# Adding every expert block's rows to X on the tensor engine in the second mixture-of-experts layer

## The chip, the cores and the metric

The kernel runs on one core of one Trainium2 chip as one launch. The core has a tensor engine (PE, with its weight loads shown apart as PEld), a vector engine (DVE), a scalar engine (ACT), GpSimd (POOL) and a sync engine (SP) that here only issues DMAs; POOL issues the indirect DMAs. The metric is device time in microseconds (us), the median of three timed runs; lower is better. Besides those runs there is one profiled execution, and all durations below come from its trace.

## The reference, cut to what matters

Two transformer blocks run one after the other on 512 tokens of width 1024. The first block has two layers, and each ends in a mixture of experts with 32 experts, of which every token uses two. In the first layer 768 rows (512 tokens and 256 context rows) go through the experts, in the second layer 512.

```python
def expert_block(args):
    xblk, e = args
    return (jax.nn.silu(xblk @ w_gate[e]) * (xblk @ w_up[e])) @ w_down[e]
...
return jnp.zeros((n_tok + 1, d), h.dtype).at[row_tok].add(yb * row_w[:, None])[:n_tok]
...
x = x + g2 * hier_moe(h2.reshape(b * s, d), *moe).reshape(x.shape)
```

So each expert multiplies its tokens' rows by three float32 matrices (1024x512, 1024x512, 512x1024, 6.3 MB together), the result is scaled by the routing weight, and the two results of each token are added to the residual stream X after a multiplication by the column g2.

## The kernel before, in words

`moe(l, n_tok, fg, side_work)` is called once per layer. The experts are ranked by load. A block holds 128 rows: either one expert with up to 128 rows (a single), or two experts with 64 rows each (a pair), which run as two column halves of PE at `tile_position` (0, 0) and (0, 64). In the second layer there are 18 blocks: block 0 is a pair, 1 to 4 are singles (`MANY = 4`), 5 to 17 are pairs. The list `turn` sets the order in which they run; the loop over `e` goes through it.

For each block, `expert` gathers the rows with an indirect DMA (`xg`), transposes them on PE (`xt`), and then runs three stages: gate, up and down. Each has four chunks. A chunk loads one 512 KB `raw` tile per expert (issued by SP, in a ring of reused buffers) and multiplies it in float32, which the trace shows as two instructions for one product: 8 instructions in a chunk of a pair and 4 in a chunk of a single, so 96 or 48 in a block. `h` of the gate and up stages (`eh`) is transposed on PE into `ht` for the down stage. In the loop, iteration e issues gate of e, gather and transposes of e+1, down of e-1, and up of e.

After the down stage of a block, `rows_of` scales the two result banks into `ey` (ACT) and `put` scatters the rows to a DRAM tensor `yd` by indirect DMA (line 985). Near the end `add_rows` reads `yd` back in four 1 MB pieces `yr` (line 1031), adds the two rows of each token (DVE, line 1034), transposes them on PE and adds them to X (DVE, line 1042). The last two blocks (`own`) are not sent through DRAM: `own_parts` makes `ysh` and `ysl` (a value and its rest, both in the rounded float32 form `fp32r`) and a one-hot matrix `own` of slot by token; `add_own` multiplies 128 columns of `ysh` and of `ysl` by the one-hot matrix, two PE products of 128x512 into a `tp` bank, and DVE adds the bank to X (line 1022). It does so for 8 column groups k, so 16 products per block.

Side work is woven in by `hooked`, called after each chunk: `self.hook = (n, generator)` runs n steps of the generator there. `self.pe` records an order for PE when `pe_turn` is set: each PE instruction then stands behind the one written before it; otherwise a scheduler may place it elsewhere. In iteration 12 (`pause`) stands `overflow`, a loop behind a branch that runs only for experts that hold more rows than their slots.

The FFN that follows takes over the products of the last block.

Of the kernel before, what the change touches and what calls it, by code (L numbers as in the profile page):

```python
# [59 lines left out]
class Kernel:  # L60
# [212 lines left out]
    def setup(self, ctx):  # L273
# [5 lines left out]
        self.wrings = [(pool("wsp", 3), 3, [0])]  # L279
        self.more_raw = (13, 13)  # L280
        self.open_x(ctx, 2)
# [502 lines left out]

    def overflow(self, l, n_tok, h2d, Yd, p2, x):

# [6 lines left out]
        with tc.If(nb > 0):  # L793
            with tc.For_i(0, nb, 1) as i:
                with ExitStack() as st:
# [30 lines left out]
                    *_, pss = self.expert(p2, l, [bass.ds(e, 1)], x, queue=nc.gpsimd)  # L826
                    y = self.rows_of(p2, pss, wt[:, 0:1])
                    nc.gpsimd.indirect_dma_start(
                        out=Yd, out_offset=bass.IndirectOffsetOnAxis(ap=row[:, 0:1], axis=0),
                        in_=y, in_offset=None, bounds_check=2 * n_tok - 1, oob_is_err=False)  # L830

# [6 lines left out]
    def moe(self, l, n_tok, fg, side_work):  # L838
# [7 lines left out]
        h2d = self.dram.tile([n_tok, D], F32, name=f"h2d{l}")  # L846
        Yd = self.dram.tile([2 * n_tok, D], F32, name=f"yd{l}")
        with ExitStack() as st:
# [4 lines left out]
            with ExitStack() as st1:  # L853
# [108 lines left out]

                turn = [0]
                for i in range(nb - 1 - MANY[l]):
                    turn += [1 + i] * (i < MANY[l]) + [1 + MANY[l] + i]
                pair = n1 - 2 * (1 + MANY[l])
                ranks = lambda b: [0, 1] if b == 0 else [b + 1] if b <= MANY[l] else [2 * b + pair, 2 * b + pair + 1]
                ysc = []
                with ExitStack() as st2:
# [23 lines left out]

                    def own_parts(e, pss, hot):

                        w = swt(turn[e])
                        if e == own[0]:
                            YS = self.split_tile(p2, [128, CH], "ys", 1)
                        elif len(segs) == 1:
                            YS = self.split_tile(self.turn_of(self.wrings)[0], [128, CH], "w")  # L1000
                        else:
                            YS = Split(*[p2.tile([128, CH], F32R, name=self.uid("ys"), tag="xt", bufs=2) for _ in (1, 2)])
                        for b in range(2):
                            o = slice(512 * b, 512 * b + 512)
                            nc.scalar.activation(YS.hi[:, o], pss[b], AF.Copy, scale=w)
                            V.scalar_tensor_tensor(YS.lo[:, o], pss[b], w, YS.hi[:, o].bitcast(F32), op0=ALU.mult, op1=ALU.subtract)
                        tokf = p2.tile([128, 1], F32, name=self.uid("tokf"), tag="tokf", bufs=2)
                        V.tensor_copy(tokf, stok(turn[e]))
                        V.tensor_scalar(hot, toks, tokf, None, op0=ALU.is_equal)
                        return YS, hot  # L1010

# [34 lines left out]
                    own = range(nb - 2, nb)  # L1046
                    rows = add_rows()
                    start(0)
                    last = V.memset(xg[1], 0.0)
                    nc.gpsimd.memset(xg[2], 0.0)  # L1050
                    for e in range(nb):
                        if e == 0:
                            with tc.issue_after(last.ins), tc.issue_after(after_q):
                                next(ex[e])
                        else:
                            if e == own[1]:
                                self.hook, self.pe_turn = (1, rows), True
                            next(ex[e])
                        if e + 1 < nb:
                            start(e + 1)  # L1060
                        if e:
                            pss = next(ex[e - 1])
                            if e == own[1]:
                                mine = own_parts(e - 1, pss, self.own or p2.tile([128, n_tok], F32R, name="own", tag="ey", bufs=self.eys))
                                self.hook = (2 if tt > 4 else 1, rows)
                            else:
# [4 lines left out]
                        if e == 2:  # L1071
                            with tc.issue_after(self.split_last):
                                self.extra(pool)

                            z = p2.tile([128, 2, D], F32, name="zero", tag="yr", bufs=2)[:, 0]
                            nc.gpsimd.memset(z, 0.0)
                            for i in own:
                                put(i, z)
                        if e == self.pause:
                            self.overflow(l, n_tok, h2d, Yd, p2, xg[(e + 2) % 3])  # L1080
                            self.pe_last = None
# [3 lines left out]
                    for _ in chain(rows, side_work):  # L1085
                        pass
                    later_adds = len(segs) == 1
                    adds = add_own(mine) if later_adds else iter(())
                    self.hook = (2, adds)
                    pss = next(ex[nb - 1])  # L1090
                    for _ in adds:
                        pass
                    self.hook = None
                    last = own_parts(nb - 1, pss, self.own or p2.tile([128, n_tok], F32R, name="own2", tag="ey", bufs=self.eys))
                    adds = add_own(last) if later_adds else add_own(mine, last)
                    self.in_turn = False
                    del self.rings[1:]
                    if later_adds:
                        self.pe_turn = False
# [1278 lines left out]
```

## Time and profile before

| what | value |
|---|---|
| median of 3 timed runs | 2939.95 us (2939.86 to 2944.88) |
| profiled execution | 2945.97 us |
| span of its trace | 2944.3 us |
| PE busy over the span | 2739.8 us (93%) |
| DMA mean over the span | 218 GB/s |
| mean granted PE clock | 0.970 |

A shown PE duration overlaps the next one, since products are pipelined; where a pace is wanted it is the distance between the starts of two rows. All times in the rows count from the start of the span.

### The profile page before, as it was taken

The page shows a single profiled execution, that of the slowest core. Times are in us where ns is not written, and L with a number is a line of the kernel's source. Part 1 is how long each engine was busy: PE and PEld are TensorE (multiplying, and loading weights), DVE is VectorE, ACT ScalarE, POOL GpSimd, SP SyncE. Part 2 cuts the span into 40 slices and gives each one's busy share as a digit, 9 for nine tenths or more (in the row PEclk, how much of TensorE's full clock was granted, in tenths as well). Part 3 has the DMA queues.
Part 4 walks back from the last instruction along what each step waited for, and adds up shares of the span by engine and source line. Part 5 has one row for each costly group of instructions (what it writes and reads, how often), then busy time and mean ns, then how long its engine had stood idle before and what let it go on. Part 6 is the DMA issues. An engine that isn't in the chain of part 4 may idle for free. (4 is left out here: it accounts for less than half of the span.)

```text
span 2944.3 us, 35083 instructions
## 1 busy us (share of the span) xinstructions
PE 2739.8 (93%) x12714; PEld 1796.7 (61%) x12714; DVE 1242.4 (42%) x2267; ACT 886.6 (30%) x1421; POOL 430.6 (15%) x431
## 2 busy tenths in 40 slices
PE   7989889999988999989999887999999889999998
PEld 3756644333325889754433323778888777888886
DVE  4884530000025566842100114654337767444335
ACT  3464211110103477310000002333226665333223
POOL 1663110000001100111000001550002230000000
PEclk9999989999999999989999998999999999999999
DMA  7656699999995201289999995333233422232231
GB/s 251 209 191 230 222 352 408 398 398 403 398 409 218 72 31 37 93 318 397 405 412 412 410 414 199 104 123 102 93 103 115 130 58 83 93 97 97 94 96 62
DMA packets 210850, 642.98 MB, mean 218 GB/s; under 512 B 31440, under 2 KB 40752, under 8 KB 209392
## 3 DMA queue, kind: packets, MB, share of 16 engines
q1 hardware_dynamic: 194208, 598.89, 55.1%
q0 software_dynamic: 16464, 41.80, 3.8%
q8 instruction: 101, 1.65, 0.2%
q14 instruction: 77, 0.63, 0.1%
HBM read 623.32 MB, written 36.14 MB: 224 GB/s over the span
## 5 line engine op out<-in xcount | busy, mean ns | idle before, releaser
L1129 PE MATMUL ps<-raw,xt 128*64 128x512 f32 (+1 forms) x2048 | 614.8, 608 | 18.5 <-DMA raw<-exp_w_up 13.1
L171 PE MATMUL ps<-Hh,wl 128*128 128x512 f32 (+1 forms) x1320 | 495.6, 377 | 3.2 <-DVE wl L91 3.1
L170 PE MATMUL ps<-Hl,wh 128*128 128x512 f32 (+1 forms) x1320 | 498.0, 378 | 0.1
L169 PE MATMUL ps<-Hh,wh 128*128 128x512 f32 (+1 forms) x1320 | 495.0, 381 | 2.9 <-ACT Hh L262 2.1
L1129 PEld LDWEIGHTS ps<-raw,xt 128*64 128x64 f32 (+1 forms) x2048 | 201.3, 148 | 373.8 <-issue 264.6
L89 ACT ACTIVATE wh<-raw 128x1024 fp32r<-128x1024 f32 (+1 forms) x224 | 231.6, 1040 | 583.8 <-PE ps L170 477.3
L91 DVE TENSOR_TENSOR wl<-raw,wh 128x1024 fp32r<-128x1024 f32 (+1 forms) x224 | 276.2, 1236 | 206.8 <-ACT wh L89 206.4
L1195 DVE TENSOR_TENSOR eh<-ps,eh 128x512 f32<-128x512 f32 x38 | 26.3, 692 | 758.2 <-PE ps L1129 706.8
L1129 PE MATMUL ps<-raw,ht 128*64 128x512 f32 (+1 forms) x1024 | 307.2, 599 | 5.4 <-issue 2.8
L169 PEld LDWEIGHTS ps<-Hh,wh 128*128 128x128 f32 x1320 | 248.2, 189 | 67.4 <-issue 5.0
L170 PEld LDWEIGHTS ps<-Hl,wh 128*128 128x128 f32 x1320 | 249.2, 189 | 56.1 <-issue 4.2
L171 PEld LDWEIGHTS ps<-Hh,wl 128*128 128x128 f32 x1320 | 248.5, 189 | 51.1 <-DVE wl L91 4.1
L1129 PEld LDWEIGHTS ps<-raw,ht 128*64 128x64 f32 (+1 forms) x1024 | 112.5, 146 | 182.6 <-issue 156.9
L1193 ACT ACTIVATE eh<-ps 128x512 f32<-128x512 f32 x38 | 22.7, 597 | 473.4 <-PE ps L1129 473.4
L413 POOL TENSOR_TENSOR cg<-cg,cp 128x798 f32<-128x798 f32 x60 | 120.9, 2015 | 102.1 <-ACT cp L412 94.3
L1217 ACT ACTIVATE ey<-ps,swt 128x512 f32<-128x512 f32 x64 | 42.9, 686 | 233.1 <-PE ps L1129 230.7
L985 POOL DMA_INDIRECT yd<-ey,srow x32 | 31.9, 995 | 548.1 <-ACT ey L1217 496.0
L169 PE MATMUL ps<-Gh,wh 128*128 128x512 f32 x256 | 101.1, 395 | 0.0
L171 PE MATMUL ps<-Gh,wl 128*128 128x512 f32 x256 | 101.1, 395 | 0.0
L170 PE MATMUL ps<-Gl,wh 128*128 128x512 f32 x256 | 101.1, 395 | 0.0
L1548 DVE TENSOR_TENSOR fs<-ps,fs 128x512 f32<-128x512 f32 x44 | 30.4, 691 | 143.1 <-PE ps L171 142.4
L362 PE MATMUL ps<-raw,sc 128*32 128x512 f32 x384 | 72.9, 643 | 5.2 <-DMA raw<-mod_w 5.2
(738 smaller groups left out, 3950.8 us busy)
## 6 DMA issues: line engine op xcount, KB each, us to landing
raw<-exp_w_gate SPq DMA_DIRECT2D x256, 512.0 KB, 11.0
raw<-exp_w_up SPq DMA_DIRECT2D x256, 512.0 KB, 10.6
raw<-exp_w_down SPq DMA_DIRECT2D x256, 512.0 KB, 10.9
raw<-ffn_w SPq DMA_DIRECT2D x132, 512.0 KB, 3.4
raw<-mod_w SPq DMA_DIRECT2D x96, 512.0 KB, 5.1
yr<-yd POOLq DMA_DIRECT2D x10, 1024.0 KB, 8.4
X<-xT SPq DMA_DIRECT2D x16, 384.0 KB, 7.5
raw<-w_in_ab SPq DMA_DIRECT2D x12, 512.0 KB, 6.8
```

Source lines behind the costliest of these rows:

```text
L89: self.nc.scalar.activation(dst.hi, src, AF.Copy)
L91: self.split_last = eng.tensor_tensor(dst.lo, src, dst.hi.bitcast(F32), ALU.subtract).ins
L169: mm(ps, a.hi, b.hi, start=start, stop=False)
L170: mm(ps, a.hi, b.lo, start=False, stop=False)
L171: mm(ps, a.lo, b.hi, start=False, stop=stop)
L362: nc.tensor.matmul(ps[32 * g:32 * g + 32], self.sc[:, 4 * h + g, 30 - 2 * i:62 - 2 * i], ws[g // 2][:, (g % 2) * 512:(g % 2 + 1) * 512], s ...
L413: nc.gpsimd.tensor_tensor(a, a, t, ALU.add)
L985: ysc.append(nc.gpsimd.indirect_dma_start(out=Yd, out_offset=bass.IndirectOffsetOnAxis(ap=srow(turn[e]), axis=0), in_=y, in_offset=None, b ...
L1129: i = f(*a, **kw).ins
L1195: nc.vector.tensor_tensor(h, ps, h, ALU.mult)
L1217: self.nc.scalar.activation(y[:, 512 * b:512 * b + 512], pss[b], AF.Copy, scale=wt)
L1548: V.tensor_tensor(s, ps, s, ALU.mult)
```

## The change

Only the second layer's experts change. The flag `direct` is set there (one token segment). Then `yd` and `add_rows` don't exist; after the down stage of every block `own_parts` makes `ysh`, `ysl` and the one-hot matrix (one buffer each, `self.own` for the one-hot), and `add_own` is hung on the hook with one step per chunk: 4 steps in the up stage of the next block and 4 in the gate stage after it. The last block's products go to the FFN as before. `pe_turn` is set in the whole loop except around the branch. The ring of `raw` tiles gets 17 instead of 13 buffers in this layer. The four singles stand at places 1, 5, 9 and 13 of the sequence instead of 1, 3, 5 and 7.

```diff
-        self.more_raw = (13, 13)
+        self.more_raw = (13, 17)
...
-        Yd = self.dram.tile([2 * n_tok, D], F32, name=f"yd{l}")
+
+        direct = len(segs) == 1
+        Yd = None if direct else self.dram.tile([2 * n_tok, D], F32, name=f"yd{l}")
...
                 turn = [0]
+                apart = (nb - 1 - MANY[l]) // MANY[l]
                 for i in range(nb - 1 - MANY[l]):
-                    turn += [1 + i] * (i < MANY[l]) + [1 + MANY[l] + i]
+                    single = [1 + i // apart] * (i % apart == 0 and i // apart < MANY[l])
+                    turn += single + [1 + MANY[l] + i]
...
-                    def own_parts(e, pss, hot):
-
-                        w = swt(turn[e])
-                        if e == own[0]:
+                    def own_parts(w, tok, pss, hot, at=None):
+
+                        if at is None:
                             YS = self.split_tile(p2, [128, CH], "ys", 1)
...
                         tokf = p2.tile([128, 1], F32, name=self.uid("tokf"), tag="tokf", bufs=2)
-                        V.tensor_copy(tokf, stok(turn[e]))
+                        V.tensor_copy(tokf, tok)
                         V.tensor_scalar(hot, toks, tokf, None, op0=ALU.is_equal)
                         return YS, hot
...
-                    rows = add_rows()
+                    rows = iter(()) if direct else add_rows()
+                    adds = iter(())
+                    parts_of = lambda e, *a: own_parts(swt(turn[e]), stok(turn[e]), *a)
...
-                            if e == own[1]:
-                                self.hook, self.pe_turn = (1, rows), True
+                            if e == own[1] and not direct:
+                                self.hook = (1, rows)
+                            self.pe_turn = direct or e >= own[1]
                             next(ex[e])
...
                             pss = next(ex[e - 1])
-                            if e == own[1]:
-                                mine = own_parts(e - 1, pss, self.own or p2.tile([128, n_tok], F32R, name="own", tag="ey", bufs=self.eys))
-                                self.hook = (2 if tt > 4 else 1, rows)
+                            if direct:
+                                for _ in adds:
+                                    pass
+                                adds = add_own(parts_of(e - 1, pss, self.own))
+                                self.hook = (1, adds)
...
                         if e == self.pause:
-                            self.overflow(l, n_tok, h2d, Yd, p2, xg[(e + 2) % 3])
+                            for _ in adds:
+                                pass
+                            self.hook, self.pe_turn = None, False
+                            self.overflow(l, n_tok, h2d, Yd, p2, xg[(e + 2) % 3], add if direct else None)
                             self.pe_last = None
...
-                    later_adds = len(segs) == 1
-                    adds = add_own(mine) if later_adds else iter(())
-                    self.hook = (2, adds)
                     pss = next(ex[nb - 1])
                     for _ in adds:
                         pass
                     self.hook = None
-                    last = own_parts(nb - 1, pss, self.own or p2.tile([128, n_tok], F32R, name="own2", tag="ey", bufs=self.eys))
-                    adds = add_own(last) if later_adds else add_own(mine, last)
+                    if direct:
+                        adds = add_own(parts_of(nb - 1, pss, self.own, self.turn_of(self.wrings)[0]))
```

What this does to the order of the engines' instructions, at two places. First PE, where one pair of the second layer ends its up stage and the next begins its gate stage. Before, the transposes of the `h` that has just been finished (`eh`) and of the next rows (`xg`) stand between the first products of the gate stage:

```order
L1129 MATMUL ps_10844<-raw_10871,xt_10646 64x512
L1129 MATMUL ps_10879<-raw_10880,xt_10784 64x512
L1129 MATMUL ps_10936<-ident,eh_10740 128x128 x4
L1129 MATMUL ps_11061<-ident,xg_9343 128x128 x4
L1129 MATMUL ps_10879<-raw_10882,xt_10784 64x512
L1129 MATMUL ps_10879<-raw_10880,xt_10784 64x512
L1129 MATMUL ps_10879<-raw_10882,xt_10784 64x512
L1129 MATMUL ps_11067<-ident,xg_9343 128x128 x4
```

In the change two one-hot products follow every chunk of four rows (8 instructions in the trace), and all transposes stand together at the end of the gate stage, right ahead of the down stage that needs the last of them:

```order
L1152 MATMUL ps_9942<-raw_9979,xt_9828 64x512
L1152 MATMUL ps_9942<-raw_9981,xt_9828 64x512
L1152 MATMUL ps_9942<-raw_9979,xt_9828 64x512
L1152 MATMUL ps_9942<-raw_9981,xt_9828 64x512
L1152 MATMUL ps_9987<-own,ysh_9882 128x512
L1152 MATMUL ps_9987<-own,ysl_9883 128x512
L1152 MATMUL ps_9999<-ident,xg_9343 128x128 x4
L1152 MATMUL ps_10005<-ident,xg_9343 128x128 x4
L1152 MATMUL ps_10012<-ident,eh_9768 128x128 x4
L1152 MATMUL ps_10018<-raw_10020,ht_10011 64x512
```

So 16 products per block have moved into 17 of the 18 blocks, and the down stage now stands directly behind the transposes of its own `h`.

Second DVE, around the same place (`xt` and `ht` are the copies of the transposed rows and of the transposed `h`). Before, the copy `ht` stands behind the two copies `xt`, and nothing is between them:

```order
L1195 TENSOR_TENSOR eh_11348<-ps_11452,eh_11348 128x512
L1173 TENSOR_TENSOR xt_11530<-ps_11531,xshift 128x512
L1173 TENSOR_TENSOR xt_11530<-ps_11537,xshift 128x512
L1202 COPY ht_11543<-ps_11544 128x512
L1195 TENSOR_TENSOR eh_11486<-ps_11590,eh_11486 128x512
```

In the change the addition to X for the last column group and the next block's one-hot matrix stand ahead of them:

```order
L1029 SCALAR_TENSOR_TENSOR X<-ps_10436,mod,X 128x512
L1016 TENSOR_SCALAR own<-acc,tokf_10494 128x512
L1196 TENSOR_TENSOR xt_10450<-ps_10451,xshift 128x512
L1196 TENSOR_TENSOR xt_10450<-ps_10457,xshift 128x512
L1015 CAST tokf_10885<-stok 128x1
L1225 COPY ht_10463<-ps_10464 128x512
L1013 SCALAR_TENSOR_TENSOR ysl_10489<-ps_10470,swt,ysh_10488 128x512
```

So `ht`, for which the down stage waits, has three more instructions ahead of it on DVE.

## Rows read from the trace of the kernel before

**Rows 1.** The page: the span in 40 slices, tenths busy, GB/s.

```profile
PE   7989889999988999989999887999999889999998
PEclk9999989999999999989999998999999999999999
GB/s 251 209 191 230 222 352 408 398 398 403 398 409 218 72 31 37 93 318 397 405 412 412 410 414 199 104 123 102 93 103 115 130 58 83 93 97 97 94 96 62
```

**Rows 2.** Windows of 50 us in the second layer's experts.

```profile
core 0: us, PE busy (x) PEld busy (x) DVE busy (x) ACT busy (x) POOL busy (x), PEclk, DMA share, GB/s
...
1350.00:1400.00 50.00, 49.11 (x185) 20.76 (x182) 7.64 (x12) 3.84 (x6) 4.06 (x4) 1.00 1.02 399
...
1700.00:1750.00 50.00, 43.91 (x147) 13.40 (x145) 3.18 (x5) 3.35 (x5) 3.11 (x4) 1.00 1.02 411
```

**Rows 3.** PE's timeline in the early blocks (start, us, instruction, count, idle before).

```profile
1287.52 15.79 PE L1129 MATMUL ps<-raw,xt 128*64 128x512 f32 x64 [1.95 <-issue]
...
1308.28 0.60 PE L1129 MATMUL ps<-ident,xg 128*128 128x128 f32 x4
1308.72 3.60 PE L1129 MATMUL ps<-raw,xt 128*128 128x512 f32 x8
...
1337.35 0.71 PE L1129 MATMUL ps<-ident,xg 128*128 128x128 f32 x4
1337.99 1.07 PE L1129 MATMUL ps<-raw,xt 128*64 128x512 f32 x2
...
1382.65 7.13 PE L1129 MATMUL ps<-raw,ht 128*128 128x512 f32 x16
1389.72 7.09 PE L1129 MATMUL ps<-raw,xt 128*64 128x512 f32 x32
1397.70 0.75 PE L1129 MATMUL ps<-ident,eh 128*128 128x128 f32 x4 [0.89 <-DVE eh L1195]
...
1445.43 0.75 PE L1129 MATMUL ps<-ident,eh 128*128 128x128 f32 x4 [0.89 <-DVE eh L1195]
```

**Rows 4.** DMA of the window 1300 to 1800 us: queue totals, issues.

```profile
q0 software_dynamic: 4962, 11.41, 5.8%
...
yr<-yd POOLq DMA_DIRECT2D x4, 1024.0 KB, 8.4
```

**Rows 5.** PE's timeline around the end of the last block.

```profile
1753.22 1.11 PE L1129 MATMUL ps<-ident,yr 128*128 128x128 f32 x4 [6.61 <-DVE yr L1034]
...
1787.22 1.94 PE L1129 MATMUL ps<-raw,ht 128*64 128x512 f32 x8 [0.78 <-DVE ht L1202]
1789.09 0.50 PE L1129 MATMUL ps<-own,ysh 128*128 128x512 f32 x1
1789.43 0.40 PE L1129 MATMUL ps<-own,ysl 128*128 128x512 f32 x1
1789.66 0.40 PE L1129 MATMUL ps<-own,ysh 128*128 128x512 f32 x1
1789.90 0.40 PE L1129 MATMUL ps<-own,ysl 128*128 128x512 f32 x1
1790.22 1.94 PE L1129 MATMUL ps<-raw,ht 128*64 128x512 f32 x8
...
1798.90 0.40 PE L1129 MATMUL ps<-own,ysl 128*128 128x512 f32 x1
1801.95 0.47 PE L1129 MATMUL ps<-own,wh 128*128 128x512 f32 x1 [2.65 <-DVE own L1009]
```

**Rows 6.** DVE by line and form, 1280 to 1800 us (busy, mean ns).

```profile
L1173 DVE TENSOR_TENSOR xt<-ps,xshift 128x512 f32<-128x512 f32 x36 | 23.2, 682 | 24.7 <-PE ps L1129 24.7
...
L1202 DVE COPY ht<-ps 128x512 f32<-128x512 f32 x18 | 12.3, 683 | 8.3 <-PE ps L1129 8.3
...
L1022 DVE SCALAR_TENSOR_TENSOR X<-ps,mod,X 128x512 f32<-128x512 f32 x7 | 5.0, 748 | 5.9 <-PE ps L1129 5.9
...
L1009 DVE TENSOR_SCALAR own<-acc,tokf 128x512 fp32r<-128x512 f32 x1 | 0.5, 498 | 0.0
```

**Rows 7.** The timeline at the branch of the overflow loop.

```profile
1619.53 2.06 PE L1129 MATMUL ps<-raw,xt 128*64 128x512 f32 x8 [0.51 <-PEq L793]
...
1626.90 1.94 PE L1129 MATMUL ps<-ident,xg 128*128 128x128 f32 x8 [5.31 <-DMA xg<-h2d,stok]
```

More of the change, by code (lines that the diff above doesn't have):

```diff
@@ L783, in extra, with overflow @@
         self.more = (lst, xl, at)
-    def overflow(self, l, n_tok, h2d, Yd, p2, x):
+    def overflow(self, l, n_tok, h2d, Yd, p2, x, add=None):
         tc, nc = self.tc, self.nc
@@ L826, in overflow @@
                     *_, pss = self.expert(p2, l, [bass.ds(e, 1)], x, queue=nc.gpsimd)
[L827 to L830, printed above, removed]
+                    if add:
+                        add(wt[:, 0:1], tok[:, 0:1], pss)
+                    else:
+                        y = self.rows_of(p2, pss, wt[:, 0:1])
+                        nc.gpsimd.indirect_dma_start(
+                            out=Yd, out_offset=bass.IndirectOffsetOnAxis(ap=row[:, 0:1], axis=0),
+                            in_=y, in_offset=None, bounds_check=2 * n_tok - 1, oob_is_err=False)
     pause = 12
@@ L992, in moe @@
                     nc.gpsimd.iota(toks, pattern=[[1, n_tok]], base=0, channel_multiplier=0, allow_small_or_imprecise_dtypes=True)
-                    def own_parts(e, pss, hot):
-                        w = swt(turn[e])
-                        if e == own[0]:
+                    def own_parts(w, tok, pss, hot, at=None):
+                        if at is None:
                             YS = self.split_tile(p2, [128, CH], "ys", 1)
-                        elif len(segs) == 1:
-                            YS = self.split_tile(self.turn_of(self.wrings)[0], [128, CH], "w")
+                        elif direct:
+                            YS = self.split_tile(at, [128, CH], "w")
                         else:
-                            YS = Split(*[p2.tile([128, CH], F32R, name=self.uid("ys"), tag="xt", bufs=2) for _ in (1, 2)])
+                            YS = Split(*[at.tile([128, CH], F32R, name=self.uid("ys"), tag="xt", bufs=2) for _ in (1, 2)])
                         for b in range(2):
@@ L1046, in moe, with add @@
                     own = range(nb - 2, nb)
-                    rows = add_rows()
+                    rows = iter(()) if direct else add_rows()
+                    adds = iter(())
+                    parts_of = lambda e, *a: own_parts(swt(turn[e]), stok(turn[e]), *a)
+                    def add(*a):
+                        for _ in add_own(own_parts(*a, self.own)):
+                            pass
                     start(0)
@@ L1062, in moe @@
                             pss = next(ex[e - 1])
-                            if e == own[1]:
-                                mine = own_parts(e - 1, pss, self.own or p2.tile([128, n_tok], F32R, name="own", tag="ey", bufs=self.eys))
-                                self.hook = (2 if tt > 4 else 1, rows)
+                            if direct:
[3 more added lines that the diff above has]
+                                self.hook = (1, adds)
+                            elif e == own[1]:
+                                mine = parts_of(e - 1, pss, p2.tile([128, n_tok], F32R, name="own", tag="ey", bufs=self.eys))
+                                self.hook = (2, rows)
                             else:
@@ L1073, in moe @@
                                 self.extra(pool)
[L1075 to L1078, printed above, removed]
+                            if not direct:
+                                z = p2.tile([128, 2, D], F32, name="zero", tag="yr", bufs=2)[:, 0]
+                                nc.gpsimd.memset(z, 0.0)
+                                for i in own:
+                                    put(i, z)
                         if e == self.pause:
-                            self.overflow(l, n_tok, h2d, Yd, p2, xg[(e + 2) % 3])
+                            for _ in adds:
+                                pass
+                            self.hook, self.pe_turn = None, False
+                            self.overflow(l, n_tok, h2d, Yd, p2, xg[(e + 2) % 3], add if direct else None)
                             self.pe_last = None
@@ L1093, in moe @@
                     self.hook = None
-                    last = own_parts(nb - 1, pss, self.own or p2.tile([128, n_tok], F32R, name="own2", tag="ey", bufs=self.eys))
-                    adds = add_own(last) if later_adds else add_own(mine, last)
+                    if direct:
+                        adds = add_own(parts_of(nb - 1, pss, self.own, self.turn_of(self.wrings)[0]))
+                    else:
+                        adds = add_own(mine, parts_of(nb - 1, pss, p2.tile([128, n_tok], F32R, name="own2", tag="ey", bufs=self.eys), p2))
                     self.in_turn = False
                     del self.rings[1:]
-                    if later_adds:
+                    if direct:
                         self.pe_turn = False
```

## The prediction

> **What bounds the kernel now.** I read the slices of the page first [rows 1]: two stretches run at some 400 GB/s, the experts of the two layers. Only the second, from about 1287 to 1799 us, is touched. There both PE and the DMA engines look full, and the question is which of them ends last. The windows [rows 2] answer it: in the late window the DMA engines move 411 GB/s and PE is busy 43.9 of 50 us, in the early window it is 399 GB/s with PE busy 49.1. The granted clock is 1.00 in both (the 2.4 GHz level), so no term below has a clock in it. PE's busy time hides overlap, so I take its pace from starts. In the early blocks, where singles and pairs alternate, the same transposes come back after 1445.43 - 1397.70 = 47.73 us [rows 3]; that is one single and one pair, and within it PE waits only 0.89 us. A pair's 32 instructions of one stage start at 1389.72 and end before 1396.8, the 16 of a single's stage take 1389.72 - 1382.65 = 7.07: both kinds cost PE the same, three stages of some 7.07 plus some 2 us of transposes, **23.87 us a block** (47.73 / 2) [rows 3].
>
> For the DMA engines they are not the same. A pair needs 24 tiles of 524 KB, 12.6 MB, 30.6 us at 411 GB/s; a single half of it, 15.3 us [rows 2]. So pairs are bound by the weights (PE has about 7 us to spare in each), singles by PE. Over the stage PE's own work is 18 x 23.87 = 429.7 us, and the stage lasts from 1287.5 to the last product of block 16's sums at 1799.2, 511.7 us [rows 3, 5]. Some 5 us of that are 16 one-hot products and some 5 the transposes of `yr`, so PE stands still for about 72 us. The stage is bound by the DMA stream, and the change takes bytes from the stream and gives work to PE.
>
> **What it removes.** The four reads of `yd` are 4.2 MB, and all indirect and POOL traffic of the window is 11.41 MB [rows 4]. Of the other 7.2 MB I count half as scatters (one per gather). So 7.8 MB go, 7.8 / 411 GB/s = 19 us of stream. The 6.61 us for which PE waits for the first `yr` [rows 5] go too; in a stage bound by the stream they are no further gain, since the stream runs on meanwhile.
>
> **What it adds to PE.** 17 blocks get 16 products inside the stage; block 17's stay with the FFN, as before. The trace has this very pattern once, in the last down stage [rows 5]: 8 instructions, 4 one-hot products, 8 instructions, from 1787.22 to 1790.22, 3.00 us. The products follow each other at 0.23 to 0.24 us (1789.43, 1789.66, 1789.90). 8 instructions at the pace of the stage (7.07 / 4) are 1.77, so four products cost 1.23 us, of which 4 x 0.235 = 0.94 are streaming and 0.29 the change-over from half-array float32 products to full-array ones and back. In the change a chunk gets two products, so the change-over is paid twice as often: 0.47 + 0.29 = 0.76 us per hook. In the chunks of a single the change-over is shorter: four transposes between its products take 1308.72 - 1308.28 = 0.44 us against 1337.99 - 1337.35 = 0.64 in a pair [rows 3]; I take 0.57 per hook there. Of the 136 hooks (17 x 8), 32 lie in the up and gate stages of the four singles, 5 run in a burst ahead of the branch at DVE's 0.75 us for one addition to X [rows 6], and 99 lie in pairs: 99 x 0.76 + 32 x 0.57 + 5 x 0.75 = 75.2 + 18.2 + 3.8 = **97 us**. Bounds: 17 x 4 x 1.23 = 84 (the price with four products to a hook), and 136 x 0.76 = 103.
>
> At the streaming price the Trainium skill is more generous: "TensorE: Matmul & The Clock Gate", section "Back-to-back issue gap", gives a sustained 131 ns for a product of 512 columns with its weight load, which would make 17 x 16 x 0.131 = 36 us of these products (an estimate from that page). The trace disagrees with it here, at 0.23 to 0.24 us from start to start [rows 5].
>
> **What it moves.** `pe_turn` fixes PE's order, and the transposes for the down stage now stand right ahead of it. After the last one-hot product of a gate stage DVE has to do the addition to X (0.75), the next one-hot matrix (0.50), two `xt` copies (0.68 each) and then `ht` (0.68) [rows 6], with a small cast some 3.35 us, while PE has three groups of transposes (some 0.65 each [rows 3], 1.95). PE waits some 1.6 us for `ht`, with the two signals between the engines. In the pace of 23.87 there is a wait of 0.89 in every second block [rows 3], 0.45 a block, and it goes, because `eh` is then long done. Net 1.15 us in 17 blocks, **20 us**. Bounds: 0.35 a block (the 0.78 that the last block waits for `ht` with DVE free [rows 5]), 6 us, and 2.1 a block if the signals and `xt` wait on each other, 36 us. At the last block the order stays as it is (its transposes already wait twice), some 1.5 us over the pace.
>
> For the first sum in an up stage `ysh` and `ysl` have to be made in the 1.8 us of its first chunk. ACT takes the first result bank before the down stage ends, and the two DVE operations of 0.75 end some 1.7 us after it. I cost this at nothing, and at 0.75 us x 17 = 13 if the cover is short.
>
> At the branch PE waits 0.51 us and then 5.31 for a gather that POOL issues after it [rows 7]. In the change the gate stage of a single (7.07 us) stands ahead of those transposes and covers most of the landing; I take 2.5 us in all, at most the present 8.
>
> Placing the singles apart costs PE nothing, since both kinds take the same PE time; it decides only how long the stream can run ahead. Four more buffers let it run 2.1 MB further ahead. Both cost nothing and, where PE ends last, gain nothing. DVE gets 136 additions (102 us in a stage of 550), ACT works on two banks per block as before; neither is near its limit. POOL loses its scatters, so gathers can only be earlier.
>
> **The sum.** PE's work from 1287.5 on: 429.7 + 97 + 20 + 1.5 + 2.5 = 550.7, which ends at 1838.2 against 1799.2: 39 us later. The stream would need 511.7 - 19 = 493, so PE ends last and the 19 us are lost in its shadow. Behind the stage the FFN's first weights can land and be split while PE still works, where now PE waits 2.65 us at its door [rows 5] with those splits on DVE; I count 2 us of gain. Net +37: 2945.97 + 37 = 2983 us in the profiled execution. Its time is 6.0 us over the median of the runs shown (2939.95), so the forecast for the median is **2977 us**.
>
> **The rivals.**
> 1. *The stream stays the bound.* The products fit into PE's 72 us of standing still, and the 7.8 MB come off the end: 2940 - 19 = 2921 us. For it: 411 GB/s in the late windows [rows 2] and 7 us to spare in each pair. It decides below (493 - 429.7) / 17 = 3.7 us per block for products and waits together. Against it: the products alone cost 4 x 1.23 = 4.9 in the trace [rows 5], and a single has no spare time at all (23.87 of PE against 15.3 of stream). Chance 8%. The page's 131 ns would give this outcome (2.1 us per block); by the measured spacing that page's rule has little weight.
> 2. *Only the cheap part of the costs.* Products at 84 us, the wait for `ht` at 6, no wait at the branch, 4 us gained at the FFN's door: 429.7 + 84 + 6 + 1.5 = 521.2, 9.5 - 4 = 5.5 us later, 2945 us. For it: the scheduler's order today hides most such waits. Against it: the change-over comes with each hook, and the hooks hold one step each. Chance for a result below 2957: 14%, a third of it within 0.2%.
> 3. *More waits.* The fixed order also stalls every up stage on `ysl` (13 us), `ht` costs the upper bound (16 more), the branch stays as it is (5 more): +71, 3011 us. For it: `ysh`, `ysl` and `own` have one buffer each, so nothing can be prepared far ahead. Chance of more than 3000: 11%.
>
> That the products might run elsewhere than planned is excluded by the order shown above.
>
> **Chances and range.** The forecast (2957 to 3000) has 67%, rival 1 8%, rival 2 14%, rival 3 11%. A difference of 0.2%, some 6 us, is about what a measurement of this kernel can tell from none. Faster: rival 1, 8%. Same: the third of rival 2, 5%. Slower: 87%. The range that leaves out rival 1, the low part of rival 2 and the far part of rival 3 is 2948 to 3000.
>
> **What would show it.** In the second layer's experts PE should have no wait for `raw` tiles between the second block and the last, and the stream should fall from 411 to some 201 MB of weights and 4 MB of gathers in 550 us, 370 to 375 GB/s. The distance from one block's down stage to the next should be some 31 us for pairs and 30 for singles, instead of 30.6 and less. Each pair of one-hot products should take 0.7 to 0.8 us out of the flow, and PE should stand 1.2 to 2 us before each down stage on `ht`. If instead the transfers run at 410 GB/s to the end and PE waits for them, rival 1 holds. The prediction fails on the low side if two products cost less than 0.5 us or if the wait for `ht` is hidden by the queue of products, on the high side if a wait ahead of the first sum shows in every up stage.

## The result and the profile after

The changed kernel takes 2965.54 us (median of 4 runs, 2962.17 to 2968.88), the kernel before 2941.89 us beside it (4 runs, 2939.86 to 2944.88): ratio 1.0079, 95% interval 1.0064 to 1.0094. It is slower by 23.6 us; 37 had been forecast, with the right direction and cause but too large a size.

The profiled execution took 2964.15 us, 18.2 more than that of before. In this execution untouched code before 300 us already ran 5.3 us earlier than in that of before, and the same 5.3 us are still there at the routing's last product ahead of the second layer's experts. So 18.2 + 5.3 = 23.5 us is what the changed stretch costs in these two executions; that it comes so close to the 23.6 of the medians is in part luck, since single executions of one kernel differ by more.

The page's slices of the changed kernel (as [rows 1]; tenths busy, GB/s):

```profile
PE   7989799999988999979999998999999889999998
GB/s 258 210 204 211 219 389 406 399 398 404 398 411 170 63 26 60 115 351 403 372 394 362 335 417 145 104 119 103 97 93 126 135 51 82 97 96 100 93 94 63
```

Where the stream ran at 397 to 414 GB/s through the second layer's experts, it now falls to 335 (369 GB/s as the mean from 1284 to 1820 us, where 370 to 375 had been forecast), and most of PE's digits are at 9. A window of 50 us in which the stream is held back, while PE is busy for 48.5 us (the rest is the wait described below):

```profile
core 0: us, PE busy (x) PEld busy (x) DVE busy (x) ACT busy (x) POOL busy (x), PEclk, DMA share, GB/s
1550.00:1600.00 50.00, 48.50 (x180) 18.57 (x180) 16.25 (x24) 3.35 (x5) 0.00 (x0) 1.00 0.92 336
```

PE's waits from 1284 to 1800 us (what it waited for, us in total, times, longest):

```profile
PE ps L1152 <- DVE ht L1225: 24.7, 17, 1.9
PE ps L1152 <- DVE xt L1196: 1.9, 2, 1.5
PE ps L1152 <- DMA xg<-h2d,stok: 0.7, 1, 0.7
PE ps L1152 <- PEq L794: 0.5, 1, 0.5
```

No wait for a `raw` tile is among them. The weight loads (PEld), which overlap PE's work, say the same: from 1290 to 1775 us they wait 9.6 us for `raw` tiles, in the kernel before 68.6 us. So PE ends last. PE's timeline: the first gate product, two chunks of a single, a pair, and the end of the last block:

```profile
1283.59 10.80 PE L1152 MATMUL ps<-raw,xt 128*64 128x512 f32 x36 [1.51 <-DVE xt L1196]
...
1440.22 1.88 PE L1152 MATMUL ps<-raw,xt 128*128 128x512 f32 x4
...
1442.40 1.88 PE L1152 MATMUL ps<-raw,xt 128*128 128x512 f32 x4
...
1487.38 1.05 PE L1152 MATMUL ps<-ident,xg 128*128 128x128 f32 x8
1488.39 0.75 PE L1152 MATMUL ps<-ident,eh 128*128 128x128 f32 x4
1490.64 7.09 PE L1152 MATMUL ps<-raw,ht 128*64 128x512 f32 x32 [1.50 <-DVE ht L1225]
...
1500.04 1.94 PE L1152 MATMUL ps<-raw,xt 128*64 128x512 f32 x8
...
1502.57 1.94 PE L1152 MATMUL ps<-raw,xt 128*64 128x512 f32 x8
...
1520.93 4.51 PE L1152 MATMUL ps<-raw,ht 128*64 128x512 f32 x20 [1.50 <-DVE ht L1225]
...
1817.58 0.40 PE L1152 MATMUL ps<-own,ysl 128*128 128x512 f32 x1
1819.41 0.47 PE L1152 MATMUL ps<-own,wh 128*128 128x512 f32 x1 [1.43 <-DVE own L1016]
...
1822.91 0.79 PE L1152 MATMUL ps<-own,wh 128*128 128x512 f32 x1 [2.33 <-DVE X L1029]
```

The new wait stands ahead of each down stage (`ht`). One pair takes 1520.93 - 1490.64 = 30.29 us. In it a chunk with its two products takes 1502.57 - 1500.04 = 2.53; less 1.77 for the chunk, a hook costs 0.76. Without its 8 hooks and its wait the block would take 30.29 - 8 x 0.76 - 1.50 = 22.7 us. DVE's timeline at the same place shows why `ht` is late:

```profile
1487.58 0.75 DVE L1029 SCALAR_TENSOR_TENSOR X<-ps,mod,X 128x512 f32<-128x512 f32 x1 [1.79 <-PE ps L1152]
1488.25 0.48 DVE L1016 TENSOR_SCALAR own<-acc,tokf 128x512 fp32r<-128x512 f32 x1
1488.64 1.28 DVE L1196 TENSOR_TENSOR xt<-ps,xshift 128x512 f32<-128x512 f32 x2
1489.84 0.15 DVE L1015 CAST tokf<-stok 128x1 f32<-128x1 int32 x1
1489.90 0.68 DVE L1225 COPY ht<-ps 128x512 f32<-128x512 f32 x1
```

PE's last transpose ends at 1489.14, but DVE is on the addition, the one-hot matrix and the two `xt` until 1489.9.

For comparing versions I use one length: from the first gate product to the first product of the last block's sum, the first row of the timeline above and its row with the wait of 1.43. In the changed kernel that is 1819.41 - 1283.59 = 535.8 us; before, from [rows 3] and [rows 5], 1801.95 - 1287.52 = 514.4. All versions (ratio to the kernel before, measured beside it):

| version | median us | ratio (95%) | length of the stage, us |
|---|---|---|---|
| before | 2940.9 to 2943.8 | 1 | 514.4 |
| changed | 2965.54 | 1.0079 (1.0064 to 1.0094) | 535.8 |
| e1_hi_only | 2938.55 | 0.9983 (0.9970 to 0.9997) | 506.7 |
| e2_two_per_hook | 2942.26 | 0.9999 (0.9985 to 1.0012) | 508.8 |
| e3_free_order | 2984.09 | 1.0135 (1.0109 to 1.0161) | 551.4 |
| e4_no_dram_rows | 2920.44 | 0.9928 (0.9900 to 0.9956) | 491.4 |
| e5_old_turn_ring | 2967.51 | 1.0085 (1.0072 to 1.0098) | 535.2 |
| v3_one_early_h | 2936.99 | 0.9985 (0.9976 to 0.9994) | 504.9 |
| v1_two_early_h | 2926.48 | 0.9949 (0.9935 to 0.9963) | 492.1 |
| v2_four_early_h | 2924.34 | 0.9937 (0.9924 to 0.9950) | 490.8 |
| e6_early_h_alone | 2940.58 | 0.9988 (0.9978 to 0.9999) | 509.2 |
| e7_v1_old_turn | 2929.26 | 0.9948 (0.9933 to 0.9964) | 502.8 |
| e8_v1_ring13 | 2920.23 | 0.9912 (0.9897 to 0.9928) | 492.2 |

The runs e1 to e4 shared one chip, e5 with v1 to v3 another, e6 to e8 a third. The median of before was 2943.0, 2940.9 and 2943.8 us there, and single executions of it lay between 2930.7 and 2952.8. So a difference in time between versions of different chips is uncertain by some 3 us; the ratios and the lengths of the stage carry the comparison.

### The profile page after: what moved, and what is told of

It reads as the page before. It is cut to its first block, busy times and chain, and to the rows that moved or that the text cites. A ratio compares the mean times of both kernels' runs of the same rounds, so it can differ in the third digit from the quotient of the medians.

```text
span 2962.5 us, 35613 instructions
## 1 busy us (share of the span) xinstructions
PE 2758.8 (93%) x12938; PEld 1803.1 (61%) x12938; DVE 1353.9 (46%) x2423; ACT 886.7 (30%) x1421; POOL 411.0 (14%) x408
## 5 line engine op out<-in xcount | busy, mean ns | idle before, releaser
L1152 PE MATMUL ps<-raw,xt 128*64 128x512 f32 (+1 forms) x2048 | 593.4, 608 | 12.0 <-DMA raw<-exp_w_up 8.4
L1152 PEld LDWEIGHTS ps<-raw,xt 128*64 128x64 f32 (+1 forms) x2048 | 189.1, 148 | 329.9 <-issue 269.4
L1152 PE MATMUL ps<-raw,ht 128*64 128x512 f32 (+1 forms) x1024 | 281.1, 597 | 29.1 <-DVE ht L1225 26.3
L1152 PEld LDWEIGHTS ps<-raw,ht 128*64 128x64 f32 (+1 forms) x1024 | 100.2, 146 | 188.9 <-issue 146.3
L1029 DVE SCALAR_TENSOR_TENSOR X<-ps,mod,X 128x512 f32<-128x512 f32 (+1 forms) x160 | 116.7, 736 | 190.2 <-PE ps L1152 190.1
L1216 ACT ACTIVATE eh<-ps 128x512 f32<-128x512 f32 x38 | 22.7, 597 | 478.3 <-PE ps L1152 478.2
L985 POOL DMA_INDIRECT xg<-h2d,stok x36 | 36.2, 1005 | 515.4 <-PE ps L1152 464.2
L1152 PEld LDWEIGHTS ps<-own,ysh 128*128 128x128 f32 x152 | 28.4, 187 | 95.7 <-issue 93.0
```

The costliest lines, as they stand in the source:

```text
L985: nc.gpsimd.indirect_dma_start(out=x, out_offset=None, in_=h2d, in_offset=bass.IndirectOffsetOnAxis(ap=stok(turn[e]), axis=0), bounds_chec ...
L1029: V.scalar_tensor_tensor(xs, ps[:, :c], self.mcol(l, 5, k, i), xs, op0=ALU.mult, op1=ALU.add)
L1152: i = f(*a, **kw).ins
L1216: nc.scalar.activation(h, ps, AF.Silu)
```

## The experiments

**Theory and rivals.** Theory: before, the stage was bound by the stream of weights and rows; in the change PE ends last, by the price of 136 hooks and the wait on `ht`. Rivals: the stream was not the bound before; the fixed order rather than the products is the cost; the places of the singles or the longer ring did it.

**Was the stream the bound before?** `e4_no_dram_rows` is the kernel before without its scatters to `yd`, the reads of it and the additions that follow; the rows of 16 blocks are missing from the result.

```diff
                     def put(...):
...
+                        if len(segs) == 1:
+                            return
...
-                    rows = add_rows()
+                    rows = iter(()) if len(segs) == 1 else add_rows()
```

> The kernel before, with the second layer's scatters to yd, its reading back, its transposes and its additions to X left out (16 blocks' rows are missing in the result); nothing on PE is added. It is the change's removal alone. Theory (the stage before was bound by the weight stream): the 7.8 MB come off the stream, 19 us less, 2922 us, and PE's wait for yr near the end is gone. Rival (those transfers were hidden, PE or something else bound the stage): less than 5 us.

Measured: 2920.44 us, 22.6 less than before. Its windows:

```profile
1400.00:1500.00 100.00, 99.96 (x375) 39.79 (x375) 10.22 (x16) 8.26 (x13) 2.97 (x3) 1.00 1.03 416
1500.00:1600.00 100.00, 95.34 (x364) 34.28 (x362) 7.45 (x12) 7.18 (x11) 1.98 (x2) 1.00 1.03 415
```

The stream stays at 415 to 416 GB/s while PE falls to 95%, and PE waits 9.2 us for `raw` tiles in 34 places. The edit also takes PE's transposes of `yr` and its wait for `yr` away, but the stream itself ends earlier: it is full up to 1780 us in the kernel before (416 GB/s, then 319 in the next 10 us) and up to 1750 in this one (415, then 331), 23 us less counted from the first gate product. The stream was the bound, and taking rows from it is worth some 20 us. 491 us is the length with the weights and gathers alone in this order of the blocks, and the mark for what follows. It is not the shortest that the stream allows: from 1300 to 1350 us it moved 370 GB/s, with PE busy throughout.

**What do the products cost?** `e1_hi_only` leaves out the products with `ysl`, so the sums lack the rest of each value.

```diff
-                        parts = [(y, hot) for YS, hot in blocks for y in (YS.hi, YS.lo)]
+                        parts = [(y, hot) for YS, hot in blocks for y in (YS.hi, YS.lo)[:1 if direct else 2]]
```

> The change with only the product with ysh in the second layer's sums; the product with ysl is left out (its part of the result is missing). Theory (PE ends last, every product lengthens the stage by its streaming time): 17 blocks x 8 products x 0.235 us = 32 us less, some 2 us more in the FFN, so 2965 - 34 = 2931 us; the pitch of a pair's chunk falls from 2.53 to about 2.30 us. Rival A (the fixed order and its waits are the cost, products fit into gaps): less than 8 us gained. Rival B (the weight stream ends last): no change.

Measured: 27 us less than the changed kernel in time, 29.1 in the stage, where 34 and 32 had been expected; both rivals fall. A chunk with one product took 2.30 us (1501.15 - 1498.85), so a product costs 2.53 - 2.30 = 0.23, and what is left of a hook, 0.76 - 0.23, is 0.53 for the first. `e2_two_per_hook` keeps all products and puts two steps in a hook, so half as many hooks have work.

```diff
-                                self.hook = (1, adds)
+                                self.hook = (2, adds)
```

> The change with two steps of the sum per hook, so that all 8 column groups are done in the up stage. Theory (the change-over between half-array float32 products and full-array products costs 0.29 us per hook, and the last addition to X stands ahead of ht on DVE): 4 hooks fewer in 17 blocks, 16 to 20 us, and the wait ahead of the down stage falls from 1.50 to about 0.8 us, 12 us: about 28 us less, 2937 us. Rival A (only the products' streaming counts): no change. Rival B (only the wait on ht counts): 12 us less.

Measured: 23 us less, as fast as before, and 5 us short of the 28 expected; more than either rival allows. Its PE timeline:

```profile
1484.69 7.09 PE L1152 MATMUL ps<-raw,ht 128*64 128x512 f32 x32 [1.05 <-DVE ht L1225]
...
1494.54 1.94 PE L1152 MATMUL ps<-raw,xt 128*64 128x512 f32 x8
1496.41 0.50 PE L1152 MATMUL ps<-own,ysh 128*128 128x512 f32 x1
1496.74 0.40 PE L1152 MATMUL ps<-own,ysl 128*128 128x512 f32 x1
1496.98 0.40 PE L1152 MATMUL ps<-own,ysh 128*128 128x512 f32 x1
1497.21 0.40 PE L1152 MATMUL ps<-own,ysl 128*128 128x512 f32 x1
1497.54 1.94 PE L1152 MATMUL ps<-raw,xt 128*64 128x512 f32 x8
...
1503.51 7.09 PE L1152 MATMUL ps<-raw,xt 128*64 128x512 f32 x32
1510.53 1.16 PE L1152 MATMUL ps<-ident,xg 128*128 128x128 f32 x8
```

A hook with four products costs 1497.54 - 1494.54 - 1.77 = 1.23 us, against 2 x 0.76 for two hooks with two: 0.29 us are saved each time. The wait on `ht` fell to 1.05 us, 0.25 more than I had expected, though no addition stood ahead of it any more.

**Is it the fixed order?** `e3_free_order` leaves the scheduler free up to the block where the kernel before fixes it.

```diff
-                            self.pe_turn = direct or e >= own[1]
+                            self.pe_turn = e >= own[1]
```

> The change without the fixed PE order in the loop before the last block. Theory: the transposes of h go back in among the gate stage's products, so the 1.50 us that PE waits ahead of each down stage go (about 25 us), but each insertion among half-array products costs a change-over (0.7 us per block, 12 us back): about 13 us less, 2952 us. Rival A (the fixed order costs nothing): no change. Rival B (the scheduler also gathers the one-hot products into fewer groups): up to 25 us less.

Measured: 18.5 us slower than the changed kernel, where I expected 13 faster. The wait on `ht` is nearly gone (3.7 us in 3 places over the stage), as I thought; PE waits 4.6 us for a gather at the branch and 3.1 us for `ysh` instead. But I had overlooked what the scheduler does with the products. Its PE timeline:

```profile
1503.56 1.02 PE L1152 MATMUL ps<-raw,xt 128*64 128x512 f32 x2
1504.54 0.96 PE L1152 MATMUL ps<-own,ysh 128*128 128x512 f32 x3
1505.43 1.93 PE L1152 MATMUL ps<-raw,xt 128*64 128x512 f32 x6
```

It cuts the chunks into pieces of 2 and 6. Two instructions of a chunk that stand alone take 0.98 us here (1504.54 - 1503.56), where two of an unbroken run take 0.44 (7.02 / 16, from the 32 of e2 above, 1510.53 - 1503.51). The fixed order saves more than its wait costs. That wait then has to go by the order itself, which `v3_one_early_h` does: the transposes of `eh` and the copy `ht` move to the gate stage's second chunk.

```diff
+                            if direct:
+                                self.mid = ex[e - 1]
                             next(ex[e])
...
                             pss = next(ex[e - 1])
...
+                if self.mid and c == 1:
+                    next(self.mid)
+                    self.mid = None
                 self.hooked()
...
         nc.vector.tensor_copy(HT, ps.rearrange("p (k s) -> p k s", k=4))
+        yield
```

> The changed kernel with one thing moved: the four transposes of eh, and with them the copy ht, stand behind the second chunk of the next block's gate stage, ahead of that chunk's one-hot products, instead of at the end of that stage. Theory (the fixed order puts ht on the path, 1.45 us in each of 17 blocks): that wait goes, 25 us, and no change-over of PE is added, since the transposes stand beside products of the same kind: 2965.5 - 25 = 2941 us, 2938 to 2947, equal to the kernel before. Rival (the wait only moves, to xt ahead of the up stage or to ysl): 2960 us or more, with a new wait of 1 us or more in each block.

Measured: 28.6 us less than the changed kernel, 30.9 in the stage; 25 had been expected. Its PE timeline:

```profile
1482.85 7.09 PE L1158 MATMUL ps<-raw,ht 128*64 128x512 f32 x32
...
1502.38 1.94 PE L1158 MATMUL ps<-raw,xt 128*64 128x512 f32 x8
1504.25 0.75 PE L1158 MATMUL ps<-ident,eh 128*128 128x128 f32 x4
1504.76 0.48 PE L1158 MATMUL ps<-own,ysh 128*128 128x512 f32 x1
...
1510.36 1.05 PE L1158 MATMUL ps<-ident,xg 128*128 128x128 f32 x8
1511.35 7.09 PE L1158 MATMUL ps<-raw,ht 128*64 128x512 f32 x32
```

The down stage starts without a wait, and a pair takes 28.50 us instead of 30.29: 1.50 of the wait and 0.29 besides. No other wait took its place, so the rival falls.

**Does a break cost the same whoever makes it?** `e6_early_h_alone` has the same instructions as v3, with the four transposes in the middle of the third chunk.

```diff
                 for k in range(2):
+                    if self.mid and c == 2 and k == 1:
+                        next(self.mid)
+                        self.mid = None
...
-                if self.mid and c == 1:
-                    next(self.mid)
-                    self.mid = None
```

> As the version with one step to a hook and the transposes of eh moved forward, but these four transposes stand alone in the middle of the third chunk, between its half-array products, instead of beside that of the second chunk's one-hot products. The same instructions, one break more in each block. Theory (what costs is each break in the run of half-array products, whichever instruction makes it, and this is why the blocks of before, with three groups of transposes among their products, had a slower pace than I should have taken): 0.3 us in each of 17 blocks, so a period of a pair of 28.8 us instead of 28.50, and some 5 us on the time, 2942 us against 2937. Rival (the transposes' place doesn't matter, only the one-hot products pay a change-over): 28.5 us and 2937 us, plus or minus 2.

In the trace the theory holds. Its PE timeline:

```profile
1482.85 7.09 PE L1158 MATMUL ps<-raw,ht 128*64 128x512 f32 x32
...
1504.92 1.08 PE L1158 MATMUL ps<-raw,xt 128*64 128x512 f32 x4
1505.93 0.75 PE L1158 MATMUL ps<-ident,eh 128*128 128x128 f32 x4
1506.61 1.08 PE L1158 MATMUL ps<-raw,xt 128*64 128x512 f32 x4
...
1511.70 7.09 PE L1158 MATMUL ps<-raw,ht 128*64 128x512 f32 x32
```

28.85 us for the pair, 0.35 more than v3. Where the gate stage is a single's the break is free (27.08 us from 1399.15 to 1426.23, and 27.09 in v3). The stage is 4.3 us longer. The timed runs can't tell the two apart: ratios 0.9988 and 0.9985, on two chips.

**The places of the singles and the ring.** `e5_old_turn_ring` is the changed kernel without both.

```diff
-        self.more_raw = (13, 17)
+        self.more_raw = (13, 13)
...
-                    single = [1 + i // apart] * (i % apart == 0 and i // apart < MANY[l])
-                    turn += single + [1 + MANY[l] + i]
+                    turn += [1 + i] * (i < MANY[l]) + [1 + MANY[l] + i]
```

> The changed kernel with the ring of 13 buffers and the old places of the four singles (1, 3, 5, 7). Theory (PE ends last everywhere, and a single costs PE as much as a pair): the changed kernel's time, 2965.5 us plus or minus 4, and still no wait of PE for a raw tile in the stage. Rival (the four more buffers or the spreading carry the stream through the pairs): PE waits for raw tiles in the run of pairs that stands behind the last single, and the time is more than 6 us above the changed kernel's.

Measured: 2967.5 us, with the stage at 535.2 and 0.6 us of waits for `raw` tiles: no difference, as the theory says.

**Both repairs.** `v1_two_early_h` is v3 with `self.hook = (2, adds)`, `v2_four_early_h` is v3 with `(4, adds)`.

> Both repairs: two steps to a hook, and the transposes of eh moved to the second chunk of the gate stage. Theory: the version with two steps to a hook ran in 2942.3 us with 1.05 us of wait for ht in each block; these 18 us go as well, which gives 2924 us; the stream alone (2920 us in the kernel before without its rows in DRAM) is then nearly reached, so 2922 to 2930, 0.5% below the kernel before, and the first waits of PE for raw tiles show. Rival (the two steps put DVE on the path): no faster than 2936 us, with PE waiting for additions to X or for xt.

> As the version with both repairs, but with four steps to a hook, so that the change-over of PE is paid at 2 hooks in a block instead of 4. Theory: 2 x 0.29 us in each of 17 blocks, 10 us of PE, but PE would then need less than the stream, so the time stops at the stream's 2920 to 2926 us and PE waits for raw tiles. Rival (four additions of 0.75 us on DVE behind three tp banks make PE wait inside the hook, some 0.5 to 1 us at each): 2927 to 2945 us, with waits of PE for X.

v1 ran in 2926.5 us, faster than both kernels. A window of v1, and PE's waits from 1284 to 1765 us:

```profile
1400.00:1500.00 100.00, 100.00 (x404) 41.15 (x400) 39.15 (x61) 7.29 (x11) 2.97 (x3) 1.00 1.03 416
```

```profile
PE ps L1158 <- DVE xt L1202: 1.9, 2, 1.5
PE ps L1158 <- PEq L794: 0.4, 1, 0.4
```

Both are full at once: PE has nearly no wait and the stream runs at 416 GB/s. The stage is 492.1 us, against the 491.4 of e4, the mark of the stream. The waits of PE for `raw` tiles that I expected don't show. Its weight loads do wait for them, 23.4 us from 1290 to 1775 us against 9.6 in the changed kernel, but where a pair follows a pair the block takes 27.75 us to the end: PE still ends last, by next to nothing. v2 confirms the time (2924.3) but not its reason. A pair took 27.43 us (1507.49 - 1480.06) instead of v1's 27.75 (1505.60 - 1477.85), so PE saved 0.3 us a block, not 0.58, and it does not wait for the stream either. What is missing stands at the fourth step of each hook, whose two products start 0.30 and 0.34 us after the one before (1490.06, 1490.36, 1490.70) instead of 0.23; there the weight load waits 0.3 us for an addition to X. That is the rival's wait, smaller than its 0.5 to 1 us. A block with the up stage of a single even became longer (27.02 us, in v1 26.64), so the stage is only 1.3 us shorter; the intervals of v1 and v2 overlap.

**The places once more, now that both are full.** `e8_v1_ring13` is v1 with the first line of e5's edit, `e7_v1_old_turn` is v1 with the whole of it.

> The version with both repairs (2926.5 us), but with the ring of 13 buffers and the old places of the singles, 1, 3, 5 and 7, so that 10 pairs stand in a row at the end. Theory (the spreading is worth something only where PE and the stream are nearly equal, as they now are): a pair needs 12.6 MB, 30.2 us at 416 GB/s, and 27.8 us of PE; 10 pairs lose 24 us, less what the ring of 13 (6.8 MB, 16 us) has run ahead, so about 8 to 12 us more, 2935 to 2942 us, with waits of PE for raw tiles in the late pairs. Rival (the places of the singles don't matter here either, as in the changed kernel): 2926 us, plus or minus 4, without such waits.

> The version with both repairs and the new places of the singles, but with the ring of 13 buffers. Theory (between two singles stand only 3 pairs, 7 us of lag, which a ring of 13, 16 us, covers): 2926 us, plus or minus 4. Rival (the four more buffers carry it): 2932 us or more, with waits of PE for raw tiles.

These two ran on the same chip and differ only in the places of the singles: 2929.3 and 2920.2 us, 9.0 apart, with intervals that don't touch (0.9933 to 0.9964 and 0.9897 to 0.9928); the stages are 502.8 and 492.2. PE's timeline of e7, in the late pairs (the first two rows are the starts of two down stages):

```profile
1693.36 6.56 PE L1157 MATMUL ps<-raw,ht 128*64 128x512 f32 x26
...
1724.05 6.73 PE L1157 MATMUL ps<-raw,ht 128*64 128x512 f32 x26
1730.96 1.50 PE L1157 MATMUL ps<-raw,ht 128*64 128x512 f32 x5 [0.18 <-DMA raw<-exp_w_down]
```

The pair takes 1724.05 - 1693.36 = 30.69 us, where v1's and e8's pairs take 27.75, with PE waiting for `raw` tiles in it. So the order of the blocks is worth some 10 us, where PE and the stream are equal, and nothing where PE ends last. This rests on e8 beside e7 and on the lengths of the stage: the time of e7 stands below the 2935 to 2942 expected, and against v1, on another chip, it shows no loss (ratios 0.9948 and 0.9949). The ring adds nothing to the stage: e8 has v1's to 0.1 us. e8's time is 6 us below v1's all the same, below the 2922 to 2930 expected, and the intervals of their ratios don't touch. In its profiled execution the first gate product comes 1.8 us sooner after the routing's product (16.2 us against 18.0), since the transposes of the first gather now stand ahead of a wait; with the ring of 17 they stand behind it. The rest lies outside the stage and on another chip, and I leave it open.

## Why the prediction was right, and where its size was off

The stage took 534.2 us up to the last product of block 16's sums (1817.8 - 1283.59), where the sum had 550.7.

- **What bounds the kernel.** Right: e4 shows the stream's bound before, and its gain of 22.6 us where I had 19. After, PE waits for no `raw` tile, and the stream falls as forecast.
- **The products.** 0.76 us for a hook in a pair was forecast and measured. In singles I took 0.57; the pitch is 2.18 (1442.40 - 1440.22), and with 1.72 for a bare chunk of a single (two in 1527.76 - 1524.33 = 3.43 in v1) that is 0.46. 32 x 0.11 = 3.5 us too much. The Trainium skill's 131 ns a product ("TensorE: Matmul & The Clock Gate", "Back-to-back issue gap") was not seen in any version; the products stand 0.23 to 0.24 us apart.
- **The wait on `ht`.** 1.6 us forecast; 24.7 us measured in 17 waits, most of them 1.50, by the chain of DVE instructions as written: 17 x 1.6 - 24.7 = 2.5 us too much.
- **The branch.** 0.5 and 0.7 us of waits instead of the 2.5 counted.
- **The pace of a block.** This is the step that was mis-sized. The 23.87 us of [rows 3], less the wait of 0.45, are 23.42; the changed kernel's block takes 22.7 without hooks and wait. 17 x 0.71 = 12 us. The 47.73 us behind that pace hold the gate stage of one single and of one pair, and I took both kinds to cost the same. PE's timeline of before, from a single's up stage (16 of the first row's 18 instructions) through a pair's gate stage:

```profile
1413.34 8.14 PE L1129 MATMUL ps<-raw,xt 128*128 128x512 f32 x18
...
1422.58 1.93 PE L1129 MATMUL ps<-raw,xt 128*64 128x512 f32 x6
...
1425.09 5.37 PE L1129 MATMUL ps<-raw,xt 128*64 128x512 f32 x24
1430.39 7.13 PE L1129 MATMUL ps<-raw,ht 128*128 128x512 f32 x16
```

Two groups of transposes cut the pair's 32 half-array instructions into 2, 6 and 24. With 16 x 0.43 = 6.88 us for the single, the pair's gate stage takes 1430.39 - 1413.34 - 6.88 = 10.17 us. Unbroken it would be 7.02 (e2), and twelve transposes in a row take 1.76 (1489.14 - 1487.38 in the changed kernel), 8.78 together: the cuts cost 1.4 us. The single's gate stage, from the 1397.70 of [rows 3] to its down stage at 1406.27, takes 8.57 with its transposes in between, no more than 6.88 + 1.76. So 1.4 us in every second block are the 0.7. In the change all twelve transposes stand at the end of the gate stage, and no product of that stage has to be taken up again behind them. I priced this break for the one-hot products and left it in the pace of the rest, although the orders of before and after showed that the transposes move together. e6 shows that transposes pay it too, 0.35 us for one break between two pieces of four. That a cut into 2 and 6 costs about twice as much is read from the traces of before and e3; no run varied it alone.

- **The doors.** I counted 2 us gained at the FFN's door. The wait for `own` did fall from 2.65 [rows 5] to 1.43, but behind it PE waits 2.33 us for an addition to X, where it was 1.41 before: 0.3 us gained. The stage also began 1.3 us later after the routing's product (18.0 us against 16.6). The transposes of its first gather now stand behind a wait, so a memset, `tokf` and `own` of DVE come ahead of the first `xt`. In e5 and e8, with the same products but the ring of 13, it is 16.2 us, so this comes with the longer ring; I had not counted it.

Together: 37 - 12 - 3.5 - 2.5 - 1.3 + 1.7 + 1.3 = 20.7, against the 23.5 of the profiles; 2.8 us stay unassigned.

Of the rivals, the first (the stream stays the bound) falls on the waits, the third (a wait on `ysl` in every up stage) too: no such wait is in the stage. The second, cheap costs, has part of the truth in the place named above.

## What to carry to other kernels

Work that goes from a bound stream to another engine gains only up to the point where that engine ends last; add up both engines' whole stage first, and add each break that the new work makes in a run of like products, not only its streaming time. Here the change as made lost 23.6 us, and the same change with half the breaks and one group of transposes moved ahead of a wait gained 14.5 (v1). An edit that is worth nothing where one engine is the bound, as the order of the blocks was, has to be tried again when the bound moves.

## What the hardware showed

- Half-array float32 products pay some 0.3 us for an excursion to full-array products, whichever they are (0.29 with one-hot products in e2, 0.35 with transposes in e6); full-array float32 products of a single pay none (27.08 against 27.09). Where the cut leaves two of a chunk's eight instructions alone, these two take 0.98 us instead of 0.44 (e3).
- The stream held 416 GB/s while PE was busy for 100.00 of 100 us (v1, 1400 to 1500), and PE lost nothing to it: the pitch of a chunk with its four products was 2.99 us there and 3.00 in e2, with 389 GB/s from 1450 to 1500 us.
